# Rolling an 8192 x 8192 matrix: heads of 128 columns instead of 256, and the row pieces of the first 24 blocks issued as halves

## The chip, the core and the metric

The kernel runs on one core of a Trainium2 chip. Its data lie in the chip's memory (HBM); a core has 16 DMA engines that move bytes between HBM and its on-chip memory (SBUF, 128 partitions) or from HBM to HBM. DMAs are issued from queues: those of SyncE (SP) and ScalarE (ACT) are driven by hardware, that of GpSimd (POOL) by software. VectorE (DVE) does the few copies inside SBUF. The metric is the device time of one execution in microseconds (us); lower is better. Times given as a median are over several executions; the profile is of one.

## The reference

```python
def setup_inputs():
    return {
        "x": np.random.randn(8192, 8192).astype(np.float32),
        "shift": 100,
    }

def reference(x, shift):
    return np.roll(x, shift, axis=1)
```

Every row of 8192 floats (32,768 B) is moved 100 columns to the right, and its last 100 columns come round to its front: `out[r, c] = x[r, c - 100]` for c of 100 or more, and `out[r, c] = x[r, 8092 + c]` for c under 100. Nothing is computed; 268.4 MB are read and 268.4 MB are written.

## The kernel before

The shift is `s` = 100. Each output row is cut in two at column `a`, a multiple of 128: the head, columns 0 to `a` - 1, and the rest. Line 20 makes `a` = 128, lines 21 and 22 raise it to 256. `g` = `a` - `s` = 156 is how many columns of a head come from the front of the same input row.

**The rest of the rows** (lines 34 to 43) goes from HBM to HBM in DMAs issued in turn by SP and ACT (`engines` in line 25). A block `c` is 64 rows; there are 128 blocks. Within a block, `j` = 0 to 3 picks every fourth row, so one DMA has 16 rows (`e`) of columns 256 to 8191: 16 pieces of 31,744 B, 496 KB, one piece for each of the 16 DMA engines. `j` of 0 and 2 goes to SP, 1 and 3 to ACT. In the last four blocks (line 40) each such DMA is issued as two, cut at `mid` = 4224: two of 248 KB, both on the same queue. So each queue issues 248 long DMAs and then 16 halves. On each queue an issue waits until the DMA four before it has landed. Line 43 has no dependence on the heads, since the two write different columns.

**The heads** (lines 60 to 80) go through SBUF on POOL's queue. A tile `k` is 512 rows: 128 partitions with `Q` = 4 rows each; there are 16 tiles, each with buffers of its own. For each tile:

- line 72 loads `t`: for rows 1, 2 and 3 of the four of a partition, the `a` floats that begin `s` before the start of the row, so the end of the row above and the start of this one in a single piece of `a` x 4 = 1024 B. The first `s` of these are the wrapped columns of the row above, the other `g` the front of this row.
- line 73 loads the wrapped columns of row 3 (100 floats, 400 B for each partition) straight into the tile `h`;
- line 76 loads the front of row 0 (`g` floats, 624 B for each partition) straight into `h`;
- lines 74 and 77, on DVE, put the two parts of `t` in their places in `h` (rows 0 to 2 and rows 1 to 3).

When all 16 tiles' loads are issued, lines 79 and 80 store them: one DMA per tile, 512 pieces of 1024 B, to columns 0 to 255. POOL issues these in program order: three loads for each tile, then 16 stores.

Of the kernel before, what the change touches and what calls it, by code (L numbers as in the profile page):

```python
# [1 line left out]

# [4 lines left out]


@with_exitstack
def kernel(  # L10
    ctx: ExitStack,
    tc: tile.TileContext,
    x: bass.AP,
    shift: int,
    out: bass.AP,
):
    nc = tc.nc
    n_rows, n_cols = x.shape
    s = shift % n_cols
    a = -(-s // 128) * 128  # L20
    if 0 < a <= 384 and a + 128 <= n_cols:
        a += 128
    g = a - s
    P = nc.NUM_PARTITIONS
    engines = [nc.sync, nc.scalar]
    n_chunks = 16
    rows = n_rows // n_chunks

    xm = x.rearrange("(c e j) w -> c j e w", e=16, j=4)
    om = out.rearrange("(c e j) w -> c j e w", e=16, j=4)
    if a < n_cols:
        blocks = n_rows // 64
        mid = (a + n_cols) // 256 * 128
        for c in range(blocks):
            parts = ((a, mid), (mid, n_cols)) if c >= blocks - 4 and a < mid else ((a, n_cols),)  # L40
            for j in range(4):
                for lo, hi in parts:
                    engines[j % 2].dma_start(out=om[c, j, :, lo:hi], in_=xm[c, j, :, lo - s:hi - s])
    if a == 0:
        return


    if a > 512:
        for i in range(n_chunks):
            r = slice(i * rows, (i + 1) * rows)  # L50
            nc.gpsimd.dma_start(out=out[r, :s], in_=x[r, n_cols - s:])
            if g > 0:
                nc.gpsimd.dma_start(out=out[r, s:a], in_=x[r, :g])
        return

    Q = 4  # L60
    n_st = n_rows // (P * Q)
    reads = ctx.enter_context(tc.tile_pool(name="reads", bufs=n_st))
    heads = ctx.enter_context(tc.tile_pool(name="heads", bufs=n_st))
    xt = x.rearrange("(k p q) c -> k p q c", q=Q, p=P)
    ot = out.rearrange("(k p q) c -> k p q c", q=Q, p=P)
    tiles = []
    for k in range(n_st):
        t = reads.tile([P, Q - 1, a], x.dtype)
        h = heads.tile([P, Q, a], x.dtype)
        lead = bass.AP(tensor=x.tensor, offset=(k * P * Q + 1) * n_cols - s,  # L70
                       ap=[[Q * n_cols, P], [n_cols, Q - 1], [1, a]])
        nc.gpsimd.dma_start(out=t[:], in_=lead)  # L72
        nc.gpsimd.dma_start(out=h[:, Q - 1, :s], in_=xt[k, :, Q - 1, n_cols - s:])  # L73
        nc.vector.tensor_copy(h[:, :Q - 1, :s], t[:, :, :s])  # L74
        if g > 0:
            nc.gpsimd.dma_start(out=h[:, 0, s:], in_=xt[k, :, 0, :g])  # L76
            nc.vector.tensor_copy(h[:, 1:, s:], t[:, :, s:])  # L77
        tiles.append(h)
    for k, h in enumerate(tiles):
        nc.gpsimd.dma_start(out=ot[k, :, :, :a], in_=h[:])  # L80


# [1 line left out]
_INS = ['x', 'shift']  # L84
_OUTS = [((8192, 8192), 'float32')]

_NUMBERS = {'shift': 100}


# [26 lines left out]
```

## Time and profile before

| | us |
|---|---|
| time, median of 3 runs | 829.58 |
| lowest and highest run | 827.68, 831.9 |
| span of the profiled execution | 828.0 |
| POOL busy (68 instructions) | 41.3 |
| DVE busy (32 copies) | 12.3 |
| last store of heads issued, from the span's start | 379.6 |
| from issue to landing, median: t loads | 50.6 |
| from issue to landing, median: line 73's and line 76's loads | 49.9 and 43.2 |
| from issue to landing, median: stores of heads | 108.2 |
| issue of one DMA on SP, median | 0.51 |

A page of the profile has, among others: the span in 40 equal slices, with the busy share of the 16 DMA engines in tenths (9 is 90% or more) and the GB/s that they moved, counted once for each byte that a DMA moves; the DMA queues, as packets, MB, and the share of the 16 engines' time that their packets took; and the DMA issues by line, with the KB of each and the time from issue to landing. The queues' rows can be asked for any window of time. q1 and q10 are the hardware queues of SP and ACT, q0 is POOL's software queue, and q14 loads instructions. HBM's bytes on the page count reads and writes each: an HBM-to-HBM copy counts twice there and once in the queues' rows.

### The profile page before, as it was taken

The page shows a single profiled execution, that of the slowest core. Times are in us where ns is not written, and L with a number is a line of the kernel's source. Part 1 is how long each engine was busy: PE and PEld are TensorE (multiplying, and loading weights), DVE is VectorE, ACT ScalarE, POOL GpSimd, SP SyncE. Part 2 cuts the span into 40 slices and gives each one's busy share as a digit, 9 for nine tenths or more (in the row PEclk, how much of TensorE's full clock was granted, in tenths as well). Part 3 has the DMA queues.
Part 4 walks back from the last instruction along what each step waited for, and adds up shares of the span by engine and source line. Part 5 has one row for each costly group of instructions (what it writes and reads, how often), then busy time and mean ns, then how long its engine had stood idle before and what let it go on. Part 6 is the DMA issues. An engine that isn't in the chain of part 4 may idle for free. (4 is left out here: it accounts for less than half of the span.)

```text
span 828.0 us, 689 instructions
## 1 busy us (share of the span) xinstructions
DVE 12.3 (1%) x32; POOL 41.3 (5%) x68
## 2 busy tenths in 40 slices
DVE  0000000000010000000000000000000000000000
POOL 2011000000021100000000000000000000000000
DMA  9999999999999999999999999999999999999998
GB/s 308 340 350 334 344 340 337 337 339 344 337 342 348 352 351 345 354 339 346 347 341 344 333 325 325 319 330 333 330 324 322 335 330 328 322 331 328 327 314 300
DMA packets 22278, 276.90 MB, mean 334 GB/s; under 512 B 9473, under 2 KB 9729, under 8 KB 13825
## 3 DMA queue, kind: packets, MB, share of 16 engines
q1 hardware_dynamic: 8448, 130.04, 46.1%
q10 hardware_dynamic: 8448, 130.04, 44.7%
q0 software_dynamic: 5376, 16.78, 8.4%
q14 instruction: 6, 0.04, 0.0%
HBM read 268.44 MB, written 268.44 MB: 648 GB/s over the span
## 5 line engine op out<-in xcount | busy, mean ns | idle before, releaser
L80 POOL DMA_DIRECT2D out_dram<-h x16 | 11.5, 724 | 126.6 <-DMA out_dram<-h 86.8
L76 POOL DMA_DIRECT2D h<-in_x_dram x16 | 8.7, 542 | 141.4 <-DMA t<-in_x_dram 141.4
L72 POOL DMA_DIRECT2D t<-in_x_dram x16 | 12.2, 762 | 30.8 <-DMA h<-in_x_dram 30.0
L73 POOL DMA_DIRECT2D h<-in_x_dram x16 | 8.9, 559 | 39.9 <-DMA h<-in_x_dram 39.9
L74 DVE COPY h<-t 128x300 f32<-128x300 f32 x16 | 6.1, 382 | 260.2 <-DMA t<-in_x_dram 260.2
L77 DVE COPY h<-t 128x468 f32<-128x468 f32 x16 | 7.5, 467 | 0.0
L97 POOL MEMSET const-float32-0.0<- 128x1 f32 x1 | 0.1, 99 | 0.2 <-issue 0.2
L97 POOL MEMSET const-bfloat16-1.0<- 128x1 bf16 x1 | 0.1, 102 | 0.0
L97 POOL MEMSET const-float32-1.0<- 128x1 f32 x1 | 0.1, 99 | 0.0
L97 POOL MEMSET const-uint8-127<- 128x1 uint8 x1 | 0.1, 99 | 0.0
## 6 DMA issues: line engine op xcount, KB each, us to landing
out_dram<-in_x_dram ACTq DMA_DIRECT2D x248, 496.0 KB, 12.7
out_dram<-in_x_dram SPq DMA_DIRECT2D x248, 496.0 KB, 12.7
out_dram<-h POOLq DMA_DIRECT2D x16, 512.0 KB, 108.2
t<-in_x_dram POOLq DMA_DIRECT2D x16, 384.0 KB, 50.6
out_dram<-in_x_dram SPq DMA_DIRECT2D x16, 248.0 KB, 6.0
out_dram<-in_x_dram ACTq DMA_DIRECT2D x16, 248.0 KB, 5.9
h<-in_x_dram POOLq DMA_DIRECT2D x16, 78.0 KB, 43.2
h<-in_x_dram POOLq DMA_DIRECT2D x16, 50.0 KB, 49.9
```

The lines of the kernel that those rows point to most:

```text
L72: nc.gpsimd.dma_start(out=t[:], in_=lead)
L73: nc.gpsimd.dma_start(out=h[:, Q - 1, :s], in_=xt[k, :, Q - 1, n_cols - s:])
L74: nc.vector.tensor_copy(h[:, :Q - 1, :s], t[:, :, :s])
L76: nc.gpsimd.dma_start(out=h[:, 0, s:], in_=xt[k, :, 0, :g])
L77: nc.vector.tensor_copy(h[:, 1:, s:], t[:, :, s:])
L80: nc.gpsimd.dma_start(out=ot[k, :, :, :a], in_=h[:])
L97: nc = _bacc.Bacc("TRN2", target_bir_lowering=False, num_devices=1)
```

## The change

The lines that raise `a` to 256 go, so `a` = 128 and `g` = 28; and the first 24 blocks, besides the last four, are cut in two.

```diff
     a = -(-s // 128) * 128
-    if 0 < a <= 384 and a + 128 <= n_cols:
-        a += 128
     g = a - s
...
         mid = (a + n_cols) // 256 * 128
         for c in range(blocks):
-            parts = ((a, mid), (mid, n_cols)) if c >= blocks - 4 and a < mid else ((a, n_cols),)
+            parts = ((a, mid), (mid, n_cols)) if (c < 24 or c >= blocks - 4) and a < mid else ((a, n_cols),)
             for j in range(4):
                 for lo, hi in parts:
                     engines[j % 2].dma_start(out=om[c, j, :, lo:hi], in_=xm[c, j, :, lo - s:hi - s])
```

The pieces of `t` and of the stores become 512 B, those of line 76 become 112 B, and those of line 73 stay at 400 B; their number stays. A long piece is 8064 columns, 32,256 B. `mid` becomes 4096, so a row's two parts are 3968 and 4096 columns (15,872 and 16,384 B). Blocks 0 to 23 have 192 DMAs instead of 96, half of them on each of SP and ACT; each queue then issues 96 halves, 200 long DMAs and 16 halves, and still waits for the DMA four before.

## What I predict

> **What bounds the kernel now.** I read the page first: the DMA rows, the queues, the memory's bytes.
>
> ```profile
> span 828.0 us, 689 instructions
> ...
> DMA  9999999999999999999999999999999999999998
> GB/s 308 340 350 334 344 340 337 337 339 344 337 342 348 352 351 345 354 339 346 347 341 344 333 325 325 319 330 333 330 324 322 335 330 328 322 331 328 327 314 300
> ...
> q1 hardware_dynamic: 8448, 130.04, 46.1%
> q10 hardware_dynamic: 8448, 130.04, 44.7%
> q0 software_dynamic: 5376, 16.78, 8.4%
> HBM read 268.44 MB, written 268.44 MB: 648 GB/s over the span
> ```
>
> The 16 DMA engines are busy in every slice, and no compute engine matters (DVE 12.3 us, POOL 41.3 us of 828.0). q1 and q10 are the row copies of SP and ACT, HBM to HBM; q0 is the heads, HBM to SBUF and back. Busy engines leave two possible bounds: the engines themselves, or the memory behind them. The two count bytes differently: a row copy costs the memory each byte twice (read, write) and an engine once; a head byte crosses an engine twice, once on each leg, and one leg touches the memory once.
>
> To separate them I asked for the DMA queues in three windows: heads loading (20 to 240 us), heads being stored (240 to 480), row copies alone (500 to 800). First the loading:
>
> ```profile
> q10 hardware_dynamic: 2129, 33.88, 42.1%
> q1 hardware_dynamic: 2146, 33.91, 40.2%
> q0 software_dynamic: 2579, 7.04, 17.1%
> ```
>
> Storing:
>
> ```profile
> q1 hardware_dynamic: 2325, 37.11, 46.3%
> q10 hardware_dynamic: 2309, 36.61, 42.8%
> q0 software_dynamic: 2611, 9.14, 11.7%
> ```
>
> Row copies alone:
>
> ```profile
> q1 hardware_dynamic: 3110, 49.19, 50.9%
> q10 hardware_dynamic: 3104, 49.13, 48.5%
> ```
>
> Memory traffic, row copies twice and heads once: loading (2 x 67.79 + 7.04) MB / 220 us = 648.3 GB/s; storing (2 x 73.72 + 9.14) / 240 = 652.4; alone 2 x 98.32 / 300 = 655.5. It stays within 1.1%, while the engines' own bytes go from 340 through 345 to 328 GB/s. And the engine time of a row-copy MB is no constant: 82.3% of 220 us for 67.79 MB is 2.67 us, then 2.90, then 3.03 alone. The copies run faster per engine when q0 takes memory time from them. That is what a full memory path looks like, with engines that wait while they count as busy. So the memory's 536.9 MB at about 650 GB/s set the time.
>
> The Trainium skill says otherwise: the page "HBM Reference", section "Specifications (TRN2)", has a core that streams alone bounded by its 16 DMA engines, at about 425 GB/s. Here the engines move 328 GB/s on copies alone and 345 GB/s with stores mixed in, so the measurement decides against it for HBM-to-HBM copies; by that figure the change, which takes 4.19 MB net off the engines (16.78 / 2 less, 4.19 more), would be worth an estimated 4.19 / 0.425 = 9.9 us less.
>
> The halves at the end tell what halving does, by the windows view (us, DVE, POOL, clock, DMA share, GB/s); the last 16 DMAs of each queue are halves and start at about 798 us:
>
> ```profile
> 780.00:800.00 20.00, 0.00 (x0) 0.00 (x0) 1.00 1.00 325
> 800.00:820.00 20.00, 0.00 (x0) 0.00 (x0) 1.00 0.95 325
> ```
>
> And the waits of SP's DMA queue with the issues by size:
>
> ```profile
> SPq L43 <- DMA out_dram<-in_x_dram: 680.3, 260, 4.9
> ```
>
> ```profile
> out_dram<-in_x_dram SPq DMA_DIRECT2D x248, 496.0 KB, 12.7
> ...
> out_dram<-in_x_dram SPq DMA_DIRECT2D x16, 248.0 KB, 6.0
> ```
>
> Of 264 issues 260 wait for an earlier DMA: four are in flight per queue. The landing halves with the size, 12.7 to 6.0 us, so the eight in flight keep the flow at 325 GB/s.
>
> **The change part by part.** *Bytes.* Columns 128 to 255 move from the heads to the row copies. q0 loses half of 16.78 MB (-8.39 MB of memory traffic); the copies gain 8192 x 128 x 4 B = 4.19 MB, read and written (+8.39 MB). Memory traffic: 0. At 655.5 GB/s: 0 us.
>
> *Head pieces.* The count stays (6144 of t, 4096 of h, 8192 stored, 16 tiles of each); sizes fall from 1024 to 512 B for t and the stores, from 624 to 112 B for the loads of line 76, and stay 400 B for line 73. What pieces cost the memory beyond their bytes is the rate missing while they run: loading 7.2 of 655.5 GB/s over 220 us = 2.4 us, storing 3.1 of 655.5 over 240 us = 1.1 us; 3.5 us together. If that price is per byte it halves (-1.75 us), if per piece it stays (0). I take the middle, -0.9 us. Bounds: all of it goes, -3.5 us; or a 512 B piece holds the memory as long as a 1024 B one, so the 8.39 MB taken off q0 save nothing: 8.39 MB / 655.5 = +12.8 us. I stay near the first, because 1024 B pieces now run within 1.1% of the rate of 31,744 B ones, the nearest row to small pieces that there is.
>
> *Halves.* Blocks 0 to 23 issue 192 DMAs for 96: 48 more on each queue, 0.51 us each by line 43's own rows = 24 us of issuing, hidden under the 680 us in which SP's queue waits (ACT's is alike). A half goes out each 6.0 / 4 = 1.5 us per queue, so 0.51 us fits; uncovered, the 24 us would land on each queue at once. What is behind a waiting issue on SP or ACT is only the next copy. These blocks hold 24 x 64 rows x 32,256 B = 49.5 MB, twice that in memory traffic: 99.1 MB / 650 = 152 us. The halves ran at 325 GB/s against 328 in the 300 us of copies alone: -0.9%, +1.4 us; against the 20 us just before them (325 too) nothing. I take the mean, +0.7 us. Bounds: the 20 us windows of copies alone lie between 321 and 335 GB/s, so one window can hide 2%: -3 us to +3 us; and if the rate followed the DMA share (0.95 for 1.00), +7.6 us.
>
> The rule that speaks against it is in the Trainium skill, page "DMA: Bandwidth & Descriptors", section "Anatomy of one DMA — SWDGE (gpsimd) path": a DMA costs about 2.0 us fixed, plus its bytes. It is given for the other issue path. By it 96 more DMAs, eight in flight, would be an estimated 96 x 2.0 / 8 = 24 us more; the case's row, 6.0 us to landing against 12.7, shows no fixed part that size.
>
> *POOL, DVE, order.* POOL's 64 DMA issues stay; the copies of line 77 shrink (468 to 84 elements), 7.5 us of DVE in all, hidden under the copies. A load of 384 KB lands after 50.6 us where a copy of 496 KB takes 12.7, so q0's packets stand in line behind the copies' on each engine. I take it that they come up once for each packet of q1 and q10: then packets half as long let them up twice as often, loads land well under 50 us, and the heads end earlier than now (stores issue until 379.6 us and land about 108 us later). They end 340 us before the span does, so earlier is worth 0; later would cost nothing until that cover was gone. The pieces of the last four blocks are 3968 and 4096 columns instead of 3968 twice: under 0.1 us at the end.
>
> **Sum.** 828.0 - 0.9 + 0.7 = 827.8 us in the profiled execution, which lies 1.6 us under the median of 829.58. Forecast for the median: 829.5 us, its own range 825 to 834. (Today's price of the heads gone or doubled, -3.5 or +3.5, and the halves' scatter of -3 to +3, taken as independent: the root of 3.5 squared and 3 squared is 4.6, about 829.4.)
>
> **Rivals.** *Small pieces cost the memory more than bytes (slower).* Place: the 18,432 pieces on q0. Price: +12.8 + 0.7, so 843 us at full price. It decides above 4.1 us, that is from a 512 B piece that costs as much as 512 x (1 + 3.4 / 12.8) = 650 B. For it: the loading window already has the lowest memory rate, and q0 there takes 17.1% of the engines for 7.04 of 74.83 MB (9.4%), so loads are hard on something. Against: 1.1% is all that this costs today, and the stores, 9.14 of 82.88 MB, take 11.7% of the engines for 11.0% of the bytes. Chance 0.24.
>
> *Halves leave engines idle (slower).* Each queue waits for all 16 engines to finish a DMA before it issues the fourth after it; with half the bytes in flight one late engine starves the others sooner. For it: share 0.95. Against: the rate did not fall with it, and in blocks 0 to 23 q0's packets are there to fill the gap. 829.6 + 7.6 = 837 us. Chance 0.10.
>
> *The engines are the bound (faster).* Then q0's 8.4% x 828.0 = 69.6 us halves (-34.8), and 4.19 MB more on q1 and q10 cost 90.8% x 828.0 / 260.08 MB = 2.89 us per MB: +12.1. Net -22.7, so 829.6 - 22.7 + 0.7 = 808 us in full; half of it gives 819. For it: engines at 0.99 to 1.01 everywhere. Against: the three memory rates above, and a copy MB costing between 2.67 and 3.03 us of engine. Chance 0.26, most of it partial.
>
> *No change, as summed.* 0.40.
>
> **Numbers.** The three runs before spread over 4.2 us, so 0.5% (4.1 us) is about what can be told from no change. Faster 0.26, same 0.40, slower 0.24 + 0.10 = 0.34. The range goes down to 818 (half the engine rival, the full one left out) and up to 843 (the full price of pieces).
>
> **What would show it.** Right: memory traffic near 650 GB/s while heads run and 655 after, with q0 at about 8.4 MB and the heads done before 490 us. The pieces' rival: the sum 2 x (q1 + q10) + q0 falls below 640 GB/s while q0 is busy, and recovers after it. The halves' rival: DMA share below 0.97 in the first 160 us with the rate down beside it, and not after block 23. The engine rival: memory traffic above 665 GB/s once heads are smaller. I am wrong if the copies alone, after the heads, run at another rate than 655 GB/s: no step here expects that.

## The result, and the profile after

The changed kernel takes 830.36 us (median of 16 runs, 828.44 to 833.14) against 828.47 us for the kernel before beside it (16 runs, 826.85 to 831.9). The ratio is 1.0025, with a 95% interval of 1.0014 to 1.0035: some 2 us slower, a small loss but clear of no change, and no change was forecast. The two profiled executions show hardly any of it (spans of 828.3 us and 828.0 us), because the one before was itself above its median, at 829.58 us. So one trace of each can say what works differently; what it costs has to come from the repeated runs.

From the page of the changed kernel, the span, the DMA rows by slices and the queues:

```profile
span 828.3 us, 785 instructions
...
DMA  9999989999999999999999999999999999999998
GB/s 310 355 356 368 377 314 328 325 331 330 327 327 327 324 330 329 321 329 326 329 332 327 321 329 326 329 330 330 322 326 327 327 329 324 333 326 327 330 316 295
...
q1 hardware_dynamic: 9984, 132.14, 48.8%
q10 hardware_dynamic: 9984, 132.14, 46.7%
q0 software_dynamic: 3328, 8.39, 3.5%
```

The bytes moved as worked out: q0 carries half of what it did. The raised GB/s that marked the heads up to slice 24 now ends after five slices: the heads are done by about 111 us instead of 490. POOL's loads and stores land after 10.4 and 17.1 us, where they took 50.6 and 108.2:

```profile
out_dram<-h POOLq DMA_DIRECT2D x16, 256.0 KB, 17.1
t<-in_x_dram POOLq DMA_DIRECT2D x16, 192.0 KB, 10.4
```

The queues of the changed kernel while its heads run (20 to 111 us; packets, MB, share of the 16 engines):

```profile
q1 hardware_dynamic: 1567, 12.61, 38.0%
q10 hardware_dynamic: 1564, 12.60, 34.5%
q0 software_dynamic: 2814, 7.27, 26.8%
```

Counted as in the prediction (row copies twice, heads once) that is (2 x 25.21 + 7.27) MB / 91 us = 634.0 GB/s of memory traffic, not the 648 to 652 of before. Then the windows (us, DVE, POOL, clock, DMA share, GB/s):

```profile
20.00:99.00 79.00, 6.30 (x26) 31.62 (x49) 1.00 1.01 362
99.00:119.00 20.00, 0.00 (x0) 0.00 (x0) 1.00 0.92 328
119.00:139.00 20.00, 0.00 (x0) 0.00 (x0) 1.00 0.96 325
...
160.00:800.00 640.00, 0.00 (x0) 0.00 (x0) 1.00 1.00 328
```

Where the heads end while halves still run, engines stand idle for a stretch (share 0.92, then 0.96); before, the place where the heads end had a share of 1.00:

```profile
470.00:490.00 20.00, 0.00 (x0) 0.00 (x0) 1.00 1.00 321
```

From 160 to 800 us the changed kernel runs as copies alone did before: q1 and q10 move 209.66 MB in 640 us, 655.2 GB/s of memory traffic against 655.5. So the cost is to be looked for in the first 160 us.

### The profile page after: what moved, and what is told of

Same layout as the page of the kernel before. It is cut to its first block, busy times and chain, and to the rows that moved or that the text cites. A ratio compares the mean times of both kernels' runs of the same rounds, so it can differ in the third digit from the quotient of the medians.

```text
span 828.3 us, 785 instructions
## 1 busy us (share of the span) xinstructions
DVE 7.8 (1%) x32; POOL 41.3 (5%) x68
## 5 line engine op out<-in xcount | busy, mean ns | idle before, releaser
L75 DVE COPY h<-t 128x84 f32<-128x84 f32 x16 | 3.2, 201 | 0.0
## 6 DMA issues: line engine op xcount, KB each, us to landing
out_dram<-h POOLq DMA_DIRECT2D x16, 256.0 KB, 17.1
t<-in_x_dram POOLq DMA_DIRECT2D x16, 192.0 KB, 10.4
```

## The experiments

Each kernel is the kernel before with the edit shown; ratios are to the kernel before, run beside it on the same chip.

| kernel | edit | ratio | interval |
|---|---|---|---|
| before_again | none | 0.9997 | 0.9984 to 1.0011 |
| heads128, heads128_again | heads of 128 | 1.0006, 1.0004 | 0.9991 to 1.0020, 0.9991 to 1.0016 |
| halves24, halves24_again | halves, blocks 0 to 23 | 1.0046, 1.0026 | 1.0030 to 1.0061, 1.0010 to 1.0042 |
| after_again | both: the changed kernel | 1.0016 | 1.0001 to 1.0031 |
| after_trim | both, halves in blocks 0 to 13 | 1.0024 | 1.0009 to 1.0038 |
| halves_all | halves, every block | 1.0034 | 1.0017 to 1.0051 |
| halves_late, halves_late_again | halves, blocks 96 to 119 | 1.0011, 1.0009 | 0.9997 to 1.0024, 0.9996 to 1.0023 |
| one_queue | all copies on SP's queue | 1.0027 | 1.0011 to 1.0042 |
| halves24_paced | halves24, heads slowed | 1.0020 | 1.0007 to 1.0033 |
| before_spread | heads slowed | 1.0021 | 1.0007 to 1.0034 |
| quarters24 | quarters, blocks 0 to 23 | 1.0515 | 1.0492 to 1.0538 |
| quarters_late | quarters, blocks 96 to 119 | 1.0553 | 1.0531 to 1.0575 |
| long_end | no halves at the end | 1.0018 | 1.0006 to 1.0030 |
| rows32 | 32 rows to a DMA | 1.0112 | 1.0096 to 1.0128 |

### One edit at a time

heads128 drops the raise of `a`; halves24 adds the halves:

```diff
-    if 0 < a <= 384 and a + 128 <= n_cols:
-        a += 128
```
```diff
-parts = ((a, mid), (mid, n_cols)) if c >= blocks - 4 and a < mid else ((a, n_cols),)
+parts = ((a, mid), (mid, n_cols)) if (c < 24 or c >= blocks - 4) and a < mid else ((a, n_cols),)
```

halves_all has only `if a < mid` there, and after_again is the changed kernel.

> Heads of 128 columns alone, no halves in the first 24 blocks. Theory H (the halves cost the 0.25%, the smaller pieces nothing): ratio 1.000 within 0.001, memory traffic while heads run at 648 to 655 GB/s. Theory P (a 512 B piece costs the memory nearly what a 1024 B one does): ratio 1.0025 to 1.004, and the memory's rate below 645 GB/s while q0 is busy. Theory J (only heads and halves together cost): ratio 1.000, like H.

> Halves in the first 24 blocks alone, heads of 256 columns. Theory H: ratio 1.002 to 1.003, and with head packets there to fill it a DMA share near 1 in the first 150 us. Theory P: 1.000 within 0.001. Theory J: 1.000 within 0.001. Under each the heads end earlier than the 490 us of before.

> Heads of 256 columns, every block issued as halves: 124 blocks of halves more than before where the change has 24. Theory H with a price per half: 5.2 x 0.0025 = ratio 1.013. Theory H with the price only where no head packets fill the engines' gaps: 1.005 to 1.02, a DMA share of 0.90 to 0.97 after the heads end. Theories P and J: within 0.002 of 1.

> The changed kernel itself on the same chip and beside the same runs of before, for comparison with the three others: ratio 1.0014 to 1.0035 under every theory, and under H and P alike the sum of the ratios less one of heads128 and halves24 within 0.0015 of this one's.

The heads alone: 1.0006, nothing that can be told from no change. The halves alone: 1.0046, on half as many runs as the rest. Theory P, the price of small pieces, falls as the cause of the rise, although one of its signs is there: heads128's memory traffic from 20 to 160 us is (2 x 42.94 + 3.86) / 140 = 641.0 GB/s, below the 645 that was named (646.4 in the repeat further down). But H in its plain form falls too: 124 blocks of halves cost no more (1.0034) than 24. The queues of halves_all from 200 to 800 us, halves all the way and no heads, show why:

```profile
q1 hardware_dynamic: 12383, 98.24, 49.9%
q10 hardware_dynamic: 12381, 98.32, 49.7%
```

2 x 196.56 MB / 600 us = 655.2 GB/s, what long pieces have alone. A half costs no rate there. The sum rule also fails: 0.0006 + 0.0046 is over the 0.0016 of after_again, as if halves cost less beside less head traffic; but the repeats further down (1.0004 and 1.0026) take most of that away. What is left is halves *beside heads*. halves24, from 20 to 160 us, and its windows from there:

```profile
q1 hardware_dynamic: 2354, 18.65, 35.5%
q10 hardware_dynamic: 2320, 18.45, 33.1%
q0 software_dynamic: 4857, 15.28, 32.1%
```
```profile
160.00:180.00 20.00, 0.00 (x0) 0.00 (x0) 1.00 0.88 301
180.00:200.00 20.00, 0.00 (x0) 0.00 (x0) 1.00 1.02 333
```

(2 x 37.10 + 15.28) / 140 = 639.1 GB/s while the heads run, which is 140 x 16.4 / 655.5 = 3.5 us lost, no more than the 3.5 us in before's trace but in 140 us instead of 460; and then an idle stretch like that of the changed kernel. (The repeats, halves24_again and after_again, have that stretch too, but weaker: the share falls to 0.95 or 0.96.) That gave two theories: D, heads packed tightly cost memory rate, and T, a stretch of idle engines when the bytes in flight shrink.

### Halves where no heads are, tight heads without halves, and slowed heads

halves_late has `96 <= c < 120` in place of `c < 24`; one_queue puts every copy on SP; halves24_paced adds a fill of an unused tile on POOL ahead of each tile's loads and each store.

```diff
-    engines = [nc.sync, nc.scalar]
+    engines = [nc.sync, nc.sync]
```
```diff
+    pace = ctx.enter_context(tc.tile_pool(name="pace", bufs=1)).tile([P, 8192], x.dtype)
     for k in range(n_st):
+        for _ in range(1):
+            nc.gpsimd.memset(pace[:], 0.0)
         t = reads.tile([P, Q - 1, a], x.dtype)
...
+        for _ in range(1):
+            nc.gpsimd.memset(pace[:], 0.0)
         nc.gpsimd.dma_start(out=ot[k, :, :, :a], in_=h[:])
```

> Heads of 256 columns; the halves are in blocks 96 to 119, issued from about 620 us on, when the heads have been done for over 100 us. Theory D (halves cost only because they let the head packets up twice as often, which packs the heads into a third of the time and lowers the memory's rate there): ratio 1.000 within 0.0015, heads done near 490 us as before. Theory H (a half costs by itself): 1.004 to 1.005, as halves24 has.

> All row copies on SP's queue, long pieces as before, eight DMAs in flight on it, so the bytes in flight and the pieces are those of before; but a head packet now has one queue to alternate with, not two. Theory D: heads done by about 200 us or earlier, memory traffic near 640 GB/s until then, ratio 1.003 to 1.005 without a single half more. Theory H: ratio within 0.0015 of 1.

> halves24 with POOL filling an unused 128 x 8192 tile before each tile's loads and before each store, so that the heads' DMAs come at longer intervals (an estimate of 16 x 9 us twice); nothing else waits for these fills. Theory D: heads spread over 300 us or more, the rate while they run nearer to 650 GB/s, ratio 1.000 to 1.003, under halves24's 1.0046. Theory H: 1.004 to 1.005, as halves24.

Late, the halves give 1.0011, not clear of no change. one_queue reaches 1.0027 with no half more than before; its last head store is issued at 231 us instead of 380. halves24_paced gives 1.0020. These ratios lean D's way, though their intervals touch their neighbours. But D's own sign is missing in one_queue: it asked for memory traffic near 640 GB/s, and from 20 to 160 us there is (2 x 41.43 + 7.81) / 140 = 647.6, against 649.9 in the kernel before. The windows of halves_late show the stretch of theory T where its halves begin:

```profile
620.00:640.00 20.00, 0.00 (x0) 0.00 (x0) 1.00 0.89 311
640.00:660.00 20.00, 0.00 (x0) 0.00 (x0) 1.00 0.97 323
660.00:780.00 120.00, 0.00 (x0) 0.00 (x0) 1.00 1.00 330
```

It is one dip, (328 - 311) / 328 x 20 = 1.0 us, and then full rate. The repeat gives 1.0009, and its trace has the dip again (share 0.92 from 620 to 640 us). That agrees with 1 us, but neither interval excludes no change:

> The same as halves_late, which gave 1.0011. Theory T (one stretch of idle engines as halves begin, about 1 us): 1.0005 to 1.002 again. Halves free unless beside the heads: 1.000 within 0.001.

### Again, trimmed, and spread

after_trim has `c < 14` in the changed kernel, so that the halves end before the heads do; before_spread has three fills before each tile's loads and two before each store, and no halves but the last four blocks.

> The same kernel as halves24, since that ratio rests on half as many runs as the others. Theory D (head packets packed tighter cost memory rate): 1.003 to 1.006, clear of halves_late's 1.0011. Theory T (a switch to halves costs one idle stretch of about 1 us wherever it falls, and nothing else does): 1.001 to 1.002, as halves_late.

> The changed kernel with halves in blocks 0 to 13 only, about 90 us instead of 155, so that the heads' last stores run under long pieces. Theory T, with the idle stretch being engines out of step that meet the small window of halves as the heads end: the DMA share near the heads' end stays at 0.98 or more where the changed kernel had 0.905 in one 20 us window, and the ratio is 1.0 to 1.0015. Theory D: the share may recover too, but heads still dense for the first 90 us: 1.0005 to 1.0025.

> The kernel before with POOL filling an unused tile (6.95 us each as halves24_paced shows) three times before each tile's loads and twice before each store: heads spread over about 700 us, no halves but the last four blocks. Theory D: less head traffic per us costs less, ratio 0.997 to 1.000. A price per piece alone, whatever the density: 1.000 within 0.0015. If the heads end after the row copies do, above 1.002.

halves24_again gives 1.0026 and confirms a cost, nearer to 0.3% than to 0.46%. It lies just under the range that D named, and its interval isn't clear of halves_late's. The other two are misses. In after_trim the dip at the heads' end is gone, as T asked:

```profile
99.00:119.00 20.00, 0.00 (x0) 0.00 (x0) 1.00 1.03 364
119.00:139.00 20.00, 0.00 (x0) 0.00 (x0) 1.00 1.00 327
```

yet the ratio is 1.0024, no better than the changed kernel; its trace, of the slowest of its twelve runs, has a dip elsewhere (share 0.95 from 15 to 35 us). So that dip alone is not the price. And before_spread, with heads over 580 us, is not faster but 1.0021. Its memory traffic from 20 to 480 us is (2 x 143.12 + 12.80) / 460 = 650.1 GB/s, against 650.4 for the kernel before in the same window, though less of it is heads. Thinner heads than before's gain nothing, so D, as a law that runs both ways, falls. (The fills also slow DVE's copies, 467 to 7793 ns each for the larger; the heads still end some 240 us before the span does, but whether the fills cost by themselves wasn't tried. If they do, part of before_spread's 1.0021 and of halves24_paced's 1.0020 is theirs.)

### A control, and quarters

> The kernel before, as a variant of itself. Under every theory 1.000 within 0.0013. Above 1.001 it would say that the place in the rounds is worth that much, and that much would have to come off every ratio here.

> The same as heads128, which gave 1.0006. Theory that the halves are the cost: 1.000 to 1.001 again. Theory that the smaller pieces of the heads are the cost: 1.002 or more.

The kernel before against itself gives 0.9997, so nothing has to come off the other ratios; heads128 gives 1.0004 again. quarters24 and quarters_late cut the rows of 24 blocks in four:

```diff
+            if c < 24:
+                w = (n_cols - a) // 4
+                parts = tuple((a + i * w, a + (i + 1) * w) for i in range(4))
```

> Heads of 256 columns; the first 24 blocks issued as quarters of 7936 B. Theory D (tight head packets): heads done by about 110 us, the memory's rate until then 620 to 635 GB/s, ratio 1.004 to 1.007. Theory T (one idle stretch when small pieces meet engines out of step): an idle stretch near the heads' end or at the return to long pieces, ratio 1.003 to 1.006 with most of the loss in that stretch. Halves and quarters free of charge: 1.000.

> Quarters in blocks 96 to 119, long after the heads. Theory D: ratio 1.000 to 1.002, memory traffic within 1% of 655 GB/s in those blocks. Theory T: a stretch of DMA share under 0.9 as the quarters begin, 1.001 to 1.003, and nothing after it. A price per small piece: 1.004 to 1.007, as quarters24.

Neither theory had this: 5% slower, beside heads or not. A window and the issues of quarters_late from 640 to 700 us:

```profile
660.00:680.00 20.00, 0.00 (x0) 0.00 (x0) 1.00 0.81 256
```
```profile
out_dram<-in_x_dram SPq DMA_DIRECT2D x60, 124.0 KB, 4.0
out_dram<-in_x_dram ACTq DMA_DIRECT2D x60, 124.0 KB, 4.0
```

Eight DMAs of 127 KB (124 KB in units of 1024 B) are in flight, and each lands after 4.0 us: 8 x 127 / 4.0 = 254 GB/s, and 252 is what flows. This quotient does not show a limit by itself. With eight always in flight it gives the flow whatever sets it: long pieces alone, from 500 to 800 us, land after 12.4 us, 8 x 508 / 12.4 = 328 GB/s; halves alone, in halves_all, after 6.2 us, 8 x 254 / 6.2 = 328. What sets the quarters apart is the engines' share: 0.81, where both others have 0.99 to 1.00. The engines stand idle while the queues wait for a landing (SP's queue waits 24.9 of the 60 us), so with quarters some part of the landing is no engine's work, and four in flight on each queue no longer cover it. How near to that point halves are, beside heads or alone, these rows don't show; the dips to 0.88 and 0.92 in halves24 and the changed kernel would fit, which is argued and not shown. (A quarter's edges lie at multiples of 256 B, not of 512 B as the halves' do; whether that adds to it wasn't tried.)

quarters24 also shows what tight heads do, from 20 to 80 us:

```profile
q0 software_dynamic: 4253, 13.65, 59.2%
q1 hardware_dynamic: 1299, 5.17, 22.4%
q10 hardware_dynamic: 1244, 4.94, 20.5%
```

q0 takes 59.2% of the engines, and the memory traffic is (2 x 10.11 + 13.65) / 60 = 564.5 GB/s at full engine share. Beside it: 648.3 GB/s before at 17.1%, 639.1 in halves24 at 32.1%, 634.0 in the changed kernel at 26.8% with pieces half as long. So the memory's rate does fall beside very dense heads, as D has it. Whether the engines are the bound there, or a memory that takes longer over q0's small pieces, these rows don't tell apart.

### The other direction

long_end issues no halves at all; rows32 has `e=32` in both rearrangements and blocks of 128 rows, so twice the bytes in flight.

> The kernel before without halves at the end. Theory T: the stretch of DMA share 0.95 in the last 30 us goes, worth up to 1 us, but the last pieces of 31,744 B finish further apart, which costs up to one piece's 1.4 us: ratio 0.999 to 1.001. If the end halves are worth having: 1.001 to 1.003.

> The kernel before with 32 rows to a DMA: 992 KB each, half as many, and twice the bytes in flight; pieces and the packets' turns are as before. If idle engines are part of what the heads cost: DMA share at 0.99 or more throughout until the end, ratio 0.997 to 0.9995. If the loss beside the heads is the memory's or the head pieces' own: 1.000 within 0.0015. A longer drain at the end, with 496 KB halves: above 1.001.

The end halves earn their place: without them 1.0018. The wider window, the version that the runs seemed to point to, is 1.0112. Its heads do slow down (a load lands after 73.9 us), and from 400 to 700 us

```profile
q10 hardware_dynamic: 2202, 46.57, 47.4%
q1 hardware_dynamic: 2191, 46.51, 46.3%
q0 software_dynamic: 2113, 7.64, 6.6%
```

the traffic is (2 x 93.08 + 7.64) / 300 = 646.0 GB/s, with 25 GB/s of head stores in it and no engine idle; the drain adds to it (share 0.85 in its last 35 us). Why the memory gives 646 there wasn't found. No kernel of these beats the one before.

## Why the prediction was wrong

**The bound** held for copies alone: 655 GB/s in long pieces and in halves alike. It did not hold beside dense heads. The sign that I had named, the sum under 640 while q0 is busy and recovered after, is there (634.0, then 655.2). I had put it down to small pieces; halves24 has it with 1024 B pieces at 639.1 (642.0 in its repeat), so the density of q0 makes a good part of it. But a lower rate for a shorter time is not by itself a loss against before: 21.5 GB/s missing for 91 us is 3.0 us, and in the trace of before that I had read the heads cost 3.5 us in 460.

**Bytes: 0 us.** Held: halving q0's bytes moved nothing by itself.

**Heads: -0.9 us forecast.** heads128 measured +0.0006 and +0.0004, some +0.4 us, with intervals down to -0.7 us. I split the difference between a price per byte (-1.75) and per piece (0); none of the saving is seen, so per piece was nearer. The 3.5 us that I split came from one trace, and it was the dearest: of the five traces with these heads and long pieces beside them (before, before_again, long_end and both of halves_late), the same window, 20 to 480 us, loses 3.6, 2.8, 1.7, 1.6 and 1.6 us against 655.5 GB/s. The rival of small pieces at +12.8 us is excluded.

**Halves: +0.7 us forecast, and here the mechanism failed.** The changed kernel's 1.0025 less heads128's 0.0005 leaves 0.0020 x 828.5 = 1.7 us, and with 256 columns 0.0026 to 0.0046, 2.2 to 3.8 us. The direction of the term was right and its size was not, because it was priced from the last 20 us, where halves run with no heads beside them. There halves are nearly free: 655.2 GB/s over 600 us of halves_all, and 0.8 us by the two ratios of halves_late. That the heads would end early I had seen, but not that packing them into a quarter to a third of the time gives q0 27 to 32% of the engines instead of 12 to 17%. Whether "earlier is worth 0" failed with it is not shown: one_queue, with earlier heads and no halves added, costs 1.0027, but it changes the queues too.

**The sum.** I had -0.9 + 0.7 = -0.2 us, and the ratio says +2.1. By these figures 1.3 of the 2.3 us between them come from the heads' term and 1.0 from the halves', each uncertain by about 1 us; no run shows one of them alone to be the miss. That the forecast of 829.5 us lies within 1 us of the measured 830.36 is luck: the three runs of before that I started from had a median of 829.58, 1.1 us above the 828.47 of the sixteen.

**The halves' rival** came nearest: DMA share under 0.97 with a dip after the heads. At +7.6 us it was over-priced, and after_trim shows that the dip at the heads' end is not all of it.

**Cover of the issues** held: SP's queue still waited 657.8 us in total, so 24 us more of issuing are hidden. The Trainium skill's page "DMA: Bandwidth & Descriptors" (section "Anatomy of one DMA — SWDGE (gpsimd) path") has about 2.0 us fixed for each DMA of the other issue path, by which 24 us more was the estimate. The runs don't show such a loss: 124 blocks of halves cost 0.0034 x 828.4 = 2.8 us in all. My reason against it was wrong, though. The landing halved, 12.7 to 6.0 us, because the queues were full and the memory set the flow; a fixed part can hide in such a landing, and a part that doesn't shrink with the size comes out at quarters.

**What stays open.** The kept traces together place the loss roughly, though no single one resolves it. In the first 500 us the five traces with long pieces there carry 493.5 to 496.6 MB of memory traffic, and the six with halves (the changed kernel twice, after_trim, both of halves24, halves_all) 492.2 to 495.3 MB. Against 655.5 GB/s that is 4.4 us lost on average and 6.7 us; after 500 us the two groups differ by 0.3 us. How the 2.3 us divide between the lower rate beside tight heads, the idle stretch where they end and the first 20 us (2.0 us lost on average against 2.5) is not resolved. Blocks 0 to 23 have both the heads and the start of the kernel beside them, and no run has halves at the start without heads. one_queue and before_spread, at 1.0027 and 1.0021, show that there is more than one way to lose it.

## What to carry to other kernels

Price a smaller transfer in the company in which it will run, not in a stretch where it runs alone, and when something gets earlier "for nothing", ask what it displaces while it runs. For a queue with a fixed number of DMAs in flight, bytes in flight over time to landing is only the flow: a landing that halves with the size does not show that nothing in it is fixed. Whether the window is still wide enough is told by the engines' share: 1.00 with halves alone, 0.81 with quarters. A price read from one trace should be read again from another before it is split in parts: 3.5 us here was 1.6 us elsewhere. Where the memory is the bound, bytes that change route without changing their memory traffic save nothing.

## What the runs showed of the hardware that was not expected

The fall between halves and quarters is abrupt: 248 KB DMAs hold 328 GB/s, 124 KB ones 252 with a fifth of the engines' time idle. The engines moved 396 GB/s from 20 to 80 us of quarters24, against 328 with copies alone, while the memory carried only 564.5 GB/s. And doubling the bytes in flight (rows32) made the kernel 1.1% slower, with no engine idle for most of the span.
